# A mixing and expert layer on one core: zero-padded key products, a factored one-hot, and one weight block less

## The chip, the cores and the metric

The kernel runs on one core of a Trainium2 chip. The metric is the device time of one execution in microseconds (us), median of several runs. Below, PE is TensorE (matmuls), PEld its weight loads, DVE VectorE, ACT ScalarE, POOL GpSimd and SP the engine whose queue issues most DMAs.

## The reference

One layer over 512 tokens of width 1024, in float32, cut to what the change touches:

```python
h = rms_norm(x, g_norm1) * (1 + scale1) + shift1
zq, zk, zv, ziq, zik, ziw, zp, zg = split(h @ w_in)
q = rms_norm(zq, 8 heads of 64);  k = rms_norm(zk, one head of 64)
ik = rms_norm(zik, 64);           iq = ziq, 4 heads of 64
score = sum over 4 index heads of iw * relu(iq . ik / 8)      # picks 128 keys per query
attention over the picked keys, 8 heads, one shared key/value head
x = x + gate1 * (merged attention and pooling branches @ w_out)
h2 = rms_norm(x, g_norm2) * (1 + scale2) + shift2
pq = h2 @ w_peer_q              # 8 heads x 2 halves x 64
s = pq half . 128 subkeys of that half;  top 16 of each half, best 16 of their sums
expert = i1 * 128 + i2;  gate = softmax(best 16)             # 8 heads x 16 picks per token
out = x + gate2 * sum over picks of gate * gelu(h2 . u[expert]) * v[expert]
```

## The kernel before

The program has three stretches.

*Mixing* (0 to about 360 us). Weights are split into a high and a low part of a reduced-precision format, so that each product of a weight block (128 outputs, 1024 inputs, 512 tokens) is 24 matmuls of 128x512 (`passes`, lines 168 to 170; `linear` runs a block and loads the next one). Five blocks are computed first, while the adaptive-norm columns still come in (loop from line 254): index key (its 64 columns stored twice), two blocks of index queries, values with index weights, and the key (also stored twice). The four q blocks, four pool blocks and the gate blocks follow. Index scores (`scores`, lines 313 and 314) and logits (lines 432 and 433) are products of two matmuls: one with the high part of the keys, for which the 128 rows hold a head's high part in one half and its low part in the other, and one of 64 rows with the low part of the keys. `heads` makes these 128 rows from a block of two heads. `choose` masks all but the 128 best keys; its steps and the adaptive columns are handed out between blocks by `tick`. Attention runs per token block of 128 and head, with the remaining gate and lift blocks as filling.

*Selection and gates* (about 375 to 754 us). Query blocks are multiplied, `halves` gives scores against 128 subkeys of each half (64 rows each, line 843) and picks the 16 best, `pairs` makes expert numbers and gates. For three of the four token blocks the experts are done densely: `gates` builds, for every token, a 128x128 table of gates. Per 8 tokens VectorE writes two one-hots (lines 615 and 616) and two gated ones (line 621, high and low part of the gate), TensorE multiplies them per token (line 627), and ScalarE copies the result out to `st` (line 628), which goes to memory. Between the groups, steps of `dense_acts` (the products of all 16384 experts' `u` rows, lines 555 to 557, of which 59 blocks are done here) are placed in proportion by `act_until`, the same number for each of the three token blocks.

*Output* (754 us to the end). For each of 128 blocks of experts the gated activations are multiplied with `v` (line 760); the remaining `u` blocks (lines 539 to 541) run beside it, and GpSimd gathers single rows for the fourth token block. Here the order of PE, DVE and ACT is written by hand; in the first two stretches a planner orders the instructions of each engine from the program's order and its own costs. `finish` multiplies by the output gate `g2b`, which is loaded before the last mixing block and kept.

Of the kernel before, what the change touches and what calls it, by code (L numbers as in the profile page):

```python
# [9 lines left out]
F32 = mybir.dt.float32  # L10
# [38 lines left out]
UGAP = 2  # L49
SCALED = 14  # L50
# [12 lines left out]
B_IK, B_IQ, B_VW, B_K, B_Q, B_P, B_GA, B_GP = 0, 1, 3, 4, 5, 9, 13, 21  # L63
# [3 lines left out]
def layer(ctx, tc, xT, cvec, w_ada, cols, consts, w_in, w_grp, w_up, w_out, w_pq, subk, u, uT, v, out):  # L67
# [23 lines left out]
    with ExitStack() as pre:  # L91
# [80 lines left out]
        blocks = [(f"q{i}", w_in[B_Q + i], DT) for i in range(4)]  # L172
# [29 lines left out]
        with ExitStack() as mix:  # L202
# [33 lines left out]
            with tc.tile_pool(name="xp", bufs=1, reuse_waits="tile") as xp, tc.tile_pool(name="xq", bufs=1, reuse_waits="tile") as xq, \  # L236
# [17 lines left out]
                for d in range(DT):  # L254
# [40 lines left out]
            ps = linear("q0", hh, hl)  # L295
            head_norm(ikT, C_GIK, "nik")
            ikl = ak.tile([P, S], F32R, tag="lgs", name="ikl", padded_shape=[P, 16 + S])
            split(ikh, ikl, ikT)
# [7 lines left out]
            def scores(tb):  # L306
                n = (tb + 1) * P
                sc = bias[tb]
                for h in range(NIH):
                    r0 = 64 * (h % 2)  # L310
# [3 lines left out]
                    T.matmul(ps, q[r0:r0 + 64], ikl[r0:r0 + 64, :n], start=False, stop=True)  # L314
# [21 lines left out]
            qsums = pac.tile([P, S], F32, tag="pac", name="nqs")[0:NH, :]  # L336
            for i in range(4):
                nxt = linear(f"q{i + 1}" if i < 3 else "p0", hh, hl)
                if i == 0:
# [3 lines left out]
                    kh, kl = [at.tile([P, S], F32R, tag=f"iq{i}", name=f"k{i}") for i in range(2)]  # L343
                    split(kh, kl, kT)
                queries(i, ps)
# [76 lines left out]
            def attention(tb):  # L422
# [4 lines left out]
                for h in range(NH):  # L427
# [5 lines left out]
                    T.matmul(ps[:, :m], q[r0:r0 + 64], kl[r0:r0 + 64, :m], start=False, stop=True)  # L433
# [50 lines left out]
        g2b = k2.tile([P, D], F32, name="g2b")  # L484
# [7 lines left out]
        nc.sync.dma_start(out=g2b, in_=g2row.to_broadcast([P, D]))  # L492
# [76 lines left out]
    with ExitStack() as win:  # L569
# [415 lines left out]
```

## Time and profile before

| | |
|---|---|
| median of 3 runs | 1576.3 us (1570.9 to 1577.0) |
| profiled execution | 1574.86 us, of which the span is 1573.1 us |
| PE busy | 1530.7 us, 97% |
| PEld busy | 1307.4 us, 83% |
| DVE busy | 1311.7 us, 83% |
| ACT busy | 690.2 us, 44% |
| POOL busy | 324.9 us, 21% |
| mean granted TensorE clock | 0.994 of full speed |

The span runs from the first to the last instruction. Matmuls are pipelined and their ends are modelled, so the starts of matmul rows say more than their durations. Busy shares are means over stretches with different limits.

### The profile page before, as it was taken

What the parts mean: (1) busy time and instruction counts of PE and PEld (TensorE: products, weight loads), DVE (VectorE), ACT (ScalarE), POOL (GpSimd) and SP (SyncE); (2) the same over time, 40 slices, a digit from 0 to 9 for tenths busy, and PEclk for the clock granted to TensorE, in tenths of its full rate; (3) what the DMA queues carried; (4) which work ended last, traced back from release to release, by engine and by line L of the source; (5) the groups of instructions that cost most, each with busy time, mean ns of one, the idle gap of its engine ahead of it and who ended that gap; (6) DMA issues with size and microseconds to landing.
All of it is one profiled execution on the core that took longest, in us unless ns stands there. A gap on an engine that the chain in (4) does not pass through costs nothing.

```text
span 1573.1 us, 22413 instructions
## 1 busy us (share of the span) xinstructions
PE 1530.7 (97%) x7977; PEld 1307.4 (83%) x7977; DVE 1311.7 (83%) x2658; ACT 690.2 (44%) x993; POOL 324.9 (21%) x318
## 2 busy tenths in 40 slices
PE   5999999999999999999999999999999999999998
PEld 3768766786788988899878999999999999998886
DVE  8799767657899999996668888888888888888887
ACT  4543545534346666675334333333333333333332
POOL 0000000000000000000213444444444444443320
PEclk8999999999999999999999999999999999999999
DMA  8412554343135555678999999999999999998884
GB/s 312 169 58 90 206 187 131 105 175 107 68 108 174 184 181 178 207 238 279 330 322 346 328 361 327 346 358 316 361 325 351 358 317 358 322 352 316 310 307 147
DMA packets 158689, 393.91 MB, mean 250 GB/s; under 512 B 13553, under 2 KB 68465, under 8 KB 158578
## 3 DMA queue, kind: packets, MB, share of 16 engines
q1 hardware_dynamic: 121714, 258.26, 46.8%
q0 software_dynamic: 36864, 134.23, 24.2%
q8 instruction: 62, 1.02, 0.3%
q14 instruction: 49, 0.40, 0.1%
HBM read 358.75 MB, written 33.69 MB: 249 GB/s over the span
## 4 chain that ended last, share of the span: by engine, by line
PE 51%; DVE 10%; DMA 2%; ACT 1%; issue 0%; SPq 0%; ACTq 0%; DVEq 0%
PE acc L760 30%; PE pse L541 6%; PE pse L540 6%; PE pse L539 6%; DVE ule L519 2%; DVE oa L621 2%; DMA v<-v 1%; DVE on L615 1%; DVE on L616 1%; PE pse L557 1%; PE pse L556 1%; PE pse L555 1%; DMA g<-gd 0%; PE gm L627 0%; ACT vh L750 0%
## 5 line engine op out<-in xcount | busy, mean ns | idle before, releaser
L691 POOL DMA_INDIRECT ur<-u,ei x128 | 156.7, 1224 | 633.6 <-DMA g<-gd 395.3
L760 PE MATMUL acc<-vl,Wh 128*128 128x512 f32 x768 | 237.1, 390 | 1.0 <-DVE vl L752 1.0
L760 PE MATMUL acc<-vh,Wl 128*128 128x512 f32 x768 | 237.3, 390 | 0.0
L760 PE MATMUL acc<-vh,Wh 128*128 128x512 f32 x768 | 236.8, 389 | 0.0
L699 POOL DMA_INDIRECT vr<-v,ei x128 | 165.2, 1291 | 213.5 <-DVE sacc L704 185.0
L752 DVE TENSOR_TENSOR vl<-v,vh 128x1024 fp32r<-128x1024 f32 x128 | 156.8, 1225 | 59.0 <-ACT vh L750 58.8
L541 PE MATMUL pse<-h2h,ule 128*128 128x384 f32 x552 | 185.2, 336 | 0.2 <-DVE ule L519 0.2
L540 PE MATMUL pse<-h2l,uhe 128*128 128x384 f32 x552 | 184.7, 335 | 0.0
L539 PE MATMUL pse<-h2h,uhe 128*128 128x384 f32 x552 | 184.5, 334 | 0.0
L749 ACT ACTIVATE Wh<-gelu 128x384 fp32r<-128x384 f32 x106 | 55.6, 525 | 291.0 <-PE acc L760 178.3
L760 PEld LDWEIGHTS acc<-vl,Wh 128*128 128x128 f32 x768 | 143.9, 188 | 31.9 <-DVE vl L752 2.1
L760 PEld LDWEIGHTS acc<-vh,Wl 128*128 128x128 f32 x768 | 144.2, 188 | 29.9
L555 PE MATMUL pse<-h2h,uhe 128*128 128x384 f32 x472 | 166.7, 353 | 1.0 <-ACT gelu L564 1.0
L557 PE MATMUL pse<-h2h,ule 128*128 128x384 f32 x472 | 161.5, 343 | 5.3 <-DVE ule L519 5.2
L519 DVE TENSOR_TENSOR ule<-ue,uhe 128x1024 fp32r<-128x1024 f32 x128 | 155.7, 1217 | 12.0 <-ACT uhe L518 12.0
L704 DVE SCALAR_TENSOR_TENSOR sacc<-vr,wt,sacc 128x1024 f32<-128x1024 f32 x127 | 162.7, 1281 | 2.4
L760 PEld LDWEIGHTS acc<-vh,Wh 128*128 128x128 f32 x768 | 143.1, 188 | 24.6 <-ACT vh L750 0.2
L556 PE MATMUL pse<-h2l,uhe 128*128 128x384 f32 x472 | 159.8, 338 | 0.0
L518 ACT ACTIVATE uhe<-ue 128x1024 fp32r<-128x1024 f32 x128 | 134.7, 1053 | 41.4 <-PE pse L556 34.3
L693 DVE SCALAR_TENSOR_TENSOR ur<-ur,hx 128x1024 f32<-128x1024 f32 x128 | 150.6, 1218 | 0.8 <-DMA ur<-u,ei 0.7
L750 ACT ACTIVATE vh<-v 128x1024 fp32r<-128x1024 f32 x128 | 135.9, 1062 | 9.8 <-DMA v<-v 9.4
L628 ACT ACTIVATE st<-gm 128x512 f32<-128x512 f32 x96 | 101.2, 1092 | 54.2 <-PE gm L627 49.8
(412 smaller groups left out, 2757.4 us busy)
## 6 DMA issues: line engine op xcount, KB each, us to landing
ue<-uT SPq DMA_DIRECT2D x128, 512.0 KB, 5.3
v<-v SPq DMA_DIRECT2D x128, 512.0 KB, 5.8
wada<-w_ada SPq DMA_DIRECT2D x48, 512.0 KB, 4.5
gd<-st SPq DMA_DIRECT2D x24, 1024.0 KB, 5.9
g<-gd SPq DMA_DIRECT2D x48, 512.0 KB, 8.0
ad<-gelu SPq DMA_DIRECT2D x22, 192.0 KB, 4.0
wgp<-w_in SPq DMA_DIRECT2D x8, 512.0 KB, 3.6
wga<-w_in SPq DMA_DIRECT2D x8, 512.0 KB, 3.8
```

The lines of the kernel that those rows point to most:

```text
L519: V.tensor_tensor(lo, src, hi.bitcast(F32), op=ALU.subtract)
L539: T.matmul(p, hi[:, k, :], h2h[:, k, :n], start=(k == 0), stop=False)
L540: T.matmul(p, hi[:, k, :], h2l[:, k, :n], start=False, stop=False)
L541: T.matmul(p, lo[:, k, :], h2h[:, k, :n], start=False, stop=(k == DT - 1))
L555: T.matmul(ps, hi[:, k, :], h2h[:, k, :ND], start=(k == 0), stop=False)
L556: T.matmul(ps, hi[:, k, :], h2l[:, k, :ND], start=False, stop=False)
L557: T.matmul(ps, lo[:, k, :], h2h[:, k, :ND], start=False, stop=(k == DT - 1))
L691: G.indirect_dma_start(out=ur, out_offset=None, in_=u, in_offset=bass.IndirectOffsetOnAxis(ap=ei3[:, k:k + 1], axis=0))
L699: G.indirect_dma_start(out=vr, out_offset=None, in_=v, in_offset=bass.IndirectOffsetOnAxis(ap=ei3[:, k:k + 1], axis=0))
L704: V.scalar_tensor_tensor(sacc, vr, wt[:, k:k + 1], sacc, op0=ALU.mult, op1=ALU.add)
L752: V.tensor_tensor(vl, vr, vh.bitcast(F32), op=ALU.subtract)
L760: T.matmul(acc[tb][i], x[:, t], y[:, i * 512:(i + 1) * 512], start=(c == 0 and n == 0), stop=(c == NEXP - 1 and n == 2))
```

## The change

Seven edits. Index key and key are stored in one weight block, and the first q block takes the fifth place of the first loop; the next block is loaded before the constants. The low parts of the two keys are held twice, each with zeros in one half of the 128 rows, so that the second matmul of a score or logit uses 128 rows. The subkeys of both halves are held in one table with zeros, so that `halves` multiplies once per head, with 128 rows and 256 columns. In `gates` the first key is parted into a multiple of 16 and a rest; a one-hot of the 8 multiples is multiplied with the gate, per 32 tokens, and that product with a one-hot of the 16 rests gives the gated one-hot. The copy to `st` runs over tokens innermost, so that four results lie together on the write side and the PSUM side is stepped. The dense steps are placed by `FILL`. `g2b` is loaded in the output loop.

```diff
+KL = 16
+TG = 32
+FILL = (0.36, 0.72, 1.0)
-        blocks = [(f"q{i}", w_in[B_Q + i], DT) for i in range(4)]
+        blocks = [(f"q{i}", w_in[B_Q + i], DT) for i in range(1, 4)]
...
+            q0T = ak.tile([P, S], F32, tag="rel", name="q0T")
-            begin = [(B_IK, ikT), (B_IQ, iqs[:2]), (B_IQ + 1, iqs[2:]), (B_VW, vwT), (B_K, kT)]
+            begin = [(B_KK, (ikT, kT)), (B_IQ, iqs[:2]), (B_IQ + 1, iqs[2:]), (B_VW, vwT), (B_Q, q0T)]
...
+                load_next()
                 nc.sync.dma_start(out=con, in_=consts)
                 for (_, dst), acc in zip(begin, accs):
                     if isinstance(dst, list):
                         heads(dst, acc)
+                    elif isinstance(dst, tuple):
+                        for i, t in enumerate(dst):
+                            for r0 in (0, 64):
+                                A.copy(t[r0:r0 + 64], acc[64 * i:64 * i + 64])
...
-            ps = linear("q0", hh, hl)
+            def split_keys(hi, lows, src):
+
+                A.activation(hi, src, AF.Copy)
+                for j, lo in enumerate(lows):
+                    r, o = slice(64 * j, 64 * j + 64), slice(64 - 64 * j, 128 - 64 * j)
+                    A.activation(lo[o], src[o], AF.Copy, scale=0.0)
+                    V.tensor_tensor(lo[r], src[r], hi[r].bitcast(F32), op=ALU.subtract)
...
                     T.matmul(ps, q, ikh[:, :n], start=True, stop=False)
-                    T.matmul(ps, q[r0:r0 + 64], ikl[r0:r0 + 64, :n], start=False, stop=True)
+                    T.matmul(ps, q, ikl[h % 2][:, :n], start=False, stop=True)
...
                     T.matmul(ps[:, :m], q, kh[:, :m], start=True, stop=False)
-                    T.matmul(ps[:, :m], q[r0:r0 + 64], kl[r0:r0 + 64, :m], start=False, stop=True)
+                    T.matmul(ps[:, :m], q, kl[h % 2][:, :m], start=False, stop=True)
...
-        g2b = k2.tile([P, D], F32, name="g2b")
-        nc.sync.dma_start(out=g2b, in_=g2row.to_broadcast([P, D]))
...
+        tens = kp.tile([P, NEXP // KL, 8], F16, name="tens")
+        V.tensor_copy(tens, iota.rearrange("p (a b) -> p a b", b=KL)[:, :, 0:1].to_broadcast([P, NEXP // KL, 8]))
-        sk = kp.tile([P, NH, P], F32, name="sk")
+        sk = kp.tile([P, NH, 2, P], F32, name="sk")
...
+            ki = oh.tile([P, P], I32, tag="ki", name=f"ki{tb}", bufs=1)
+            V.tensor_copy(ki, keys[:, 0, :])
+            V.tensor_scalar(ki, ki, KL - 1, None, op0=ALU.bitwise_and)
+            V.tensor_copy(low, ki)
+            V.tensor_tensor(keys[:, 0, :], keys[:, 0, :], low, op=ALU.subtract)
...
+                if g * GT % TG == 0:
+                    t = g * GT
+                    rest = oh.tile([P, TG // 2, KL, 2], F16, tag="rest", name=f"rest{tb}_{g}")
+                    V.tensor_tensor(rest, numbers(TG // 2, KL), pairs(low, t, TG).to_broadcast([P, TG // 2, KL, 2]), op=ALU.is_equal)
+                    ten = oh.tile([P, NG, NA, 8], F16, tag="ten", name=f"ten{tb}_{g}")
+                    V.tensor_tensor(ten, tens.unsqueeze(1).to_broadcast([P, NG, NA, 8]), eights(keys[:, 0, :], t), op=ALU.is_equal)
+                    gt = []
+                    for i in range(2):
+                        gt.append(oh.tile([P, NG, NA, 8], F16, tag=f"gt{i}", name=f"gt{i}_{tb}_{g}"))
+                        V.tensor_tensor(gt[i], ten, eights(part[:, i, :], t), op=ALU.mult)
...
-                    V.tensor_tensor(one, numbers, pairs(keys[:, 0, :], t), op=ALU.is_equal)
...
-                        V.tensor_tensor(x, one, pairs(part[:, i, :], t), op=ALU.mult)
+                        V.tensor_tensor(x, gt[i][:, n].rearrange("p a (q j) -> p a q j", j=2).unsqueeze(3).to_broadcast([P, NA, 4, KL, 2]),
+                                        rest[:, 4 * n:4 * n + 4].unsqueeze(1).to_broadcast([P, NA, 4, KL, 2]), op=ALU.mult)
...
-                                T.matmul(ps[:, k, :], two[:, q, :, j], gated[i][:, q, :, j], start=(i == 0), stop=(i == 1))
-                        A.activation(st[:, :, t8 + t4:t8 + t4 + 4].rearrange("p e t -> p t e"), ps, AF.Copy, scale=2.0 ** -SCALED)
+                                T.matmul(ps[:, k, :], two[:, q, :, j], gated[i][:, :, q, :, j], start=(i == 0), stop=(i == 1))
+                        A.activation(st[:, :, t8 + t4:t8 + t4 + 4], ps.rearrange("p k e -> p e k"), AF.Copy, scale=2.0 ** -SCALED)
...
-                act_until(LEAD * DT + between * (tb * steps + n + 1) // (DENSE * steps))
+                f0, f1 = (FILL[tb - 1] if tb else 0.0), FILL[tb]
+                act_until(LEAD * DT + int(between * (f0 + (f1 - f0) * (n + 1) / steps)))
...
+            if a == NEXP + 2:
+                g2b = out_gate()
...
-        for i in range(2):
-            r0 = 64 * i
-            for j in range(2):
-                T.matmul(ps[:, j, :], self.pq[r0:r0 + 64, h + j, tb * P:(tb + 1) * P], self.sk[r0:r0 + 64, h + j, :],
-                         start=True, stop=True)
+        for j in range(2):
+            T.matmul(ps, self.pq[:, h + j, tb * P:(tb + 1) * P], self.sk[:, h + j], start=True, stop=True)
...
-    w = np.concatenate([ik, ik, iq, v, iw, zero, k, k, q, p, g], axis=1)
+    w = np.concatenate([ik, k, iq, v, iw, zero, q, p, g], axis=1)
```

## Rows read from the trace of the kernel before

**Rows 1.** Stretches: us, busy us of PE, PEld, DVE, ACT, POOL, clock, DMA.
```profile
56.00:180.00 124.00, 123.94 (x511) 92.49 (x510) 109.91 (x257) 56.39 (x93) 0.00 (x0) 1.00 0.28 95
180.00:300.00 120.00, 119.71 (x579) 83.41 (x579) 80.38 (x223) 62.96 (x141) 0.00 (x0) 1.00 0.47 152
...
475.00:735.00 260.00, 250.06 (x1894) 228.45 (x1893) 251.79 (x709) 172.50 (x217) 0.00 (x0) 1.00 0.65 201
...
860.00:1573.00 713.00, 707.34 (x3493) 632.96 (x3491) 599.24 (x737) 252.21 (x340) 298.13 (x233) 1.00 0.90 326
```
**Rows 2.** Chain that ended last, in order of time: start, us, what.
```profile
1412.20 149.47 PE acc L760 x659
```

**Rows 3.** PE in order of time, logits of 256 columns: start, us, instruction.
```profile
190.01 0.28 PE L432 MATMUL lg<-k,qs 128*128 128x256 f32 x1
190.22 0.38 PE L433 MATMUL lg<-k,qs 64*128 64x256 f32 x1
190.53 0.38 PE L432 MATMUL lg<-k,qs 128*128 128x256 f32 x1
190.84 0.38 PE L433 MATMUL lg<-k,qs 64*128 64x256 f32 x1
191.15 0.50 PE L169 MATMUL psga<-hl,whga 128*128 128x512 f32 x1
191.49 0.40 PE L170 MATMUL psga<-hh,wlga 128*128 128x512 f32 x1
```

**Rows 4.** The same, logits of 512 columns.
```profile
267.14 0.39 PE L432 MATMUL lg<-k,qs 128*128 128x512 f32 x1
...
268.23 0.39 PE L170 MATMUL psup<-pTh,wlup 128*128 128x512 f32 x1
```

**Rows 5.** Lines L314 and L433: durations min/median/max in ns, starts, shapes.
```profile
L314 PE MATMUL ix<-ikl,iq x12: 379/436/502, 69.6 to 82.7; 64*128 64x256 f32 x4, 64*128 64x384 f32 x4, 64*128 64x512 f32 x4
...
L433 PE MATMUL lg<-k,qs x32: 379/409/492, 180.0 to 276.2; 64*128 64x256 f32 x16, 64*128 64x384 f32 x8, 64*128 64x512 f32 x8
```

**Rows 6.** PE in order of time: first row of block q0, and the row behind its last.
```profile
56.07 0.39 PE L168 MATMUL psq<-hh,whq 128*128 128x512 f32 x1
...
61.51 1.02 PE L291 MATMUL nikps<-niksq,con 128*128 128x512 f32 x2
```

**Rows 7.** PE in order of time around key scores: eight passes, then four.
```profile
611.72 0.72 PE L843 MATMUL ks<-sk,pq 64*128 64x128 f32 x8
612.37 0.45 PE L555 MATMUL pse<-h2h,uhe 128*128 128x384 f32 x1
...
616.74 0.71 PE L843 MATMUL ks<-sk,pq 64*128 64x128 f32 x4
617.37 0.45 PE L555 MATMUL pse<-h2h,uhe 128*128 128x384 f32 x1
```

**Rows 8.** DVE groups by line and shape, 475 to 735 us: busy us, mean ns, idle before.
```profile
L621 DVE TENSOR_TENSOR oa<-on,part 128x1024 f16<-128x1024 f16 x96 | 62.5, 682 | 0.0
L519 DVE TENSOR_TENSOR ule<-ue,uhe 128x1024 fp32r<-128x1024 f32 x45 | 54.7, 1216 | 6.4 <-ACT uhe L518 6.4
L615 DVE TENSOR_TENSOR on<-irep,keys 128x1024 f16<-128x1024 f16 x48 | 32.4, 680 | 0.7 <-ACT keys L602 0.7
...
L864 DVE TENSOR_TENSOR pr<-pr 128x256 bf16<-128x256 bf16 x9 | 2.6, 287 | 0.0
...
L864 DVE TENSOR_TENSOR pr<-k_1h 128x512 bf16<-128x512 bf16 x2 | 0.8, 417 | 0.0
```

**Rows 9.** ACT groups by line and shape, whole span: busy us, mean ns, idle before.
```profile
L628 ACT ACTIVATE st<-gm 128x512 f32<-128x512 f32 x96 | 101.2, 1092 | 54.2 <-PE gm L627 49.8 <-issue 2.5 <-ACT gelu L564 1.0
...
L449 ACT COPY pT<-pt 128x512 f32<-128x512 f32 x8 | 4.6, 580 | 4.9 <-PE pt L447 4.8
```

**Rows 10.** PE's waits from 475 to 735 us: total us, times, longest.
```profile
PE gm L627 <- DVE oa L621: 5.6, 8, 1.8
PE ks L843 <- ACT kss L846: 1.2, 2, 0.8
```

More of the change, by code (lines that the diff above doesn't have):

```diff
@@ L336, in layer @@
             qsums = pac.tile([P, S], F32, tag="pac", name="nqs")[0:NH, :]
+            ps = q0T
             for i in range(4):
                 nxt = linear(f"q{i + 1}" if i < 3 else "p0", hh, hl)
+                queries(i, ps)
                 if i == 0:
@@ L342, in layer @@
                     head_norm(kT, C_GK, "nk")
-                    kh, kl = [at.tile([P, S], F32R, tag=f"iq{i}", name=f"k{i}") for i in range(2)]
-                    split(kh, kl, kT)
-                queries(i, ps)
+                    kh, *kl = [at.tile([P, S], F32R, tag=f"iq{i}", name=f"k{i}") for i in range(3)]
+                    split_keys(kh, kl, kT)
                 tick(2)
@@ L599, in gates @@
             keys = oh.tile([P, 2, P], F16, tag="keys", name=f"keys{tb}", bufs=1)
+            low = oh.tile([P, P], F16, tag="low", name=f"low{tb}", bufs=1)
             part = oh.tile([P, 2, P], F16, tag="part", name=f"part{tb}", bufs=1)
@@ L605, in gates @@
             V.tensor_tensor(part[:, 1, :], gs, part[:, 0, :], op=ALU.subtract)
-            full = [P, 4, NEXP, 2]
-            pairs = lambda x, t: x[:, t:t + 8].rearrange("p (q j) -> p q j", j=2).unsqueeze(2).to_broadcast(full)
-            numbers = irep.unsqueeze(1).to_broadcast(full)
+            ki = oh.tile([P, P], I32, tag="ki", name=f"ki{tb}", bufs=1)
+            V.tensor_copy(ki, keys[:, 0, :])
+            V.tensor_scalar(ki, ki, KL - 1, None, op0=ALU.bitwise_and)
+            V.tensor_copy(low, ki)
@@ L610, in gates @@
+            V.tensor_tensor(keys[:, 0, :], keys[:, 0, :], low, op=ALU.subtract)
+            NA, NG = NEXP // KL, TG // 8
+            pairs = lambda x, t, n: x[:, t:t + n].rearrange("p (q j) -> p q j", j=2).unsqueeze(2)
+            numbers = lambda q, n: irep[:, :n, :].unsqueeze(1).to_broadcast([P, q, n, 2])
+            eights = lambda x, t: x[:, t:t + TG].rearrange("p (g x) -> p g x", x=8).unsqueeze(2).to_broadcast([P, NG, NA, 8])
             for g in range(P // GT):
                 st = oh.tile([P, NEXP, GT], F32, tag="st", name=f"st{tb}_{g}", bufs=STB)
+                if g * GT % TG == 0:
[8 more added lines that the diff above has]
+                        V.tensor_tensor(gt[i], ten, eights(part[:, i, :], t), op=ALU.mult)
@@ L612, in gates @@
                 for t8 in range(0, GT, 8):
                     t = g * GT + t8
-                    one, two = [oh.tile(full, F16, tag=f"on{i}", name=f"on{i}_{tb}_{t}") for i in range(2)]
-                    V.tensor_tensor(one, numbers, pairs(keys[:, 0, :], t), op=ALU.is_equal)
-                    V.tensor_tensor(two, numbers, pairs(keys[:, 1, :], t), op=ALU.is_equal)
+                    full = [P, 4, NEXP, 2]
+                    two = oh.tile(full, F16, tag="on1", name=f"on1_{tb}_{t}")
+                    V.tensor_tensor(two, numbers(4, NEXP), pairs(keys[:, 1, :], t, 8).to_broadcast(full), op=ALU.is_equal)
@@ L705, in sparse, with finish @@
             yield
-    def finish(tb, x, i, half):
+    def finish(g2b, tb, x, i, half):
         c = slice(i * 512, (i + 1) * 512)
@@ L712, in finish, with out_gate @@
         nc.sync.dma_start(out=out[tb * P:(tb + 1) * P, c], in_=x[:, c])
+    def out_gate():
+        t = up.tile([P, DT, P], F32, tag="uh", name="g2b").rearrange("p k e -> p (k e)")
+        nc.sync.dma_start(out=t, in_=g2row.to_broadcast([P, D]))
+        return t
     def residual(tb):
@@ L800, in layer @@
                 for i in range(2):
-                    finish(DENSE, x, i, sacc[:, i * 512:(i + 1) * 512])
+                    finish(g2b, DENSE, x, i, sacc[:, i * 512:(i + 1) * 512])
             if c < NEXP - 2:
@@ L811, in layer @@
                 for i in halves:
-                    finish(tb, xs[tb], i, acc[tb][i])
+                    finish(g2b, tb, xs[tb], i, acc[tb][i])
 class ProductKeys:
@@ L929, in _blocks, with _subkeys @@
     return np.ascontiguousarray(w.reshape(k // P, P, n // P, P).transpose(2, 1, 0, 3))
+def _subkeys(k):
+    s = np.zeros((2, 64, NH, 2, P), k.dtype)
+    for i in range(2):
+        s[i, :, :, i, :] = k[:, i].transpose(2, 0, 1)
+    return s.reshape(P, NH, 2, P)
 def _cols(v):
@@ L965, in arrange @@
         "w_pq": _blocks(w_peer_q[0]),
[L966 removed]
+        "subk": _subkeys(peer_subkeys[0]),
         "u": peer_u[0],
```

20 lines of the change are left out of this document (10 added, 10 removed).

## The prediction

> **What bounds the kernel now.** I read the busy shares by stretch first. TensorE is busy in 123.9 of the 124 us from 56 to 180, in 119.7 of the 120 us of the attention stretch, and in 707 of the last 713 us [rows 1]. A busy matmul row can hide waiting, so I check it by starts. Near the end 659 full matmuls of 512 columns on the critical chain take 149.47 us, 0.227 us each [rows 2], which is 512 columns at the full clock plus 14 ns. From about 860 us nothing but TensorE counts, and the change touches almost nothing there: whatever is won or lost before the first product of the dense output (start at about 754 us) is carried to the end one for one. So the question is how much earlier that point is reached.
>
> Before it there are two kinds of stretch. From 56 to 300 us TensorE never waits by the rows, but it does not always run at 0.227: where a product with 64 rows stands between products with 128 rows, starts are further apart [rows 3, 4]. VectorE is busy 109.9 of 124 us from 56 to 180 and 80.4 of 120 after that, so it is no firm limit there [rows 1]. From 475 to 735 us (the gate tables) VectorE is busy 251.8 of 260 us and TensorE 250.1 [rows 1]: both are near the wall, and the 9.9 us in which TensorE stands still are mostly waits for VectorE's gated one-hots [rows 10].
>
> **The change part by part.**
>
> *Keys in one block.* Index key and key share one weight block, and block q0 goes into the first five. Five blocks still pass through the loop before 56 us, with the same loads and splits, so that part stays. What falls away is the separate q0 after it: 24 matmuls that run from 56.07 to 61.51 us [rows 6], 5.4 us of TensorE time, and one load and one split. The evacuation grows by two half copies and a copy of q0, some 0.6 us each by the ScalarE copy of 128x512 [rows 9], about 1.8 us on an engine that is busy 56 of 124 us there [rows 1]; TensorE has block q1 to run meanwhile. "Next block split early" is what makes that true: its load is issued ahead of the constants on SP's queue, and its split no longer waits for the first `linear`. If q1 were late anyway, a split (1.2 us on VectorE [rows 8]) and ScalarE's part would show, at most 2.5 us. I take 5.4, bounds 3 and 5.4.
>
> *Products over 128 partitions with zeros.* The second half of each score and logit pair now uses all 128 rows with a half of zeros. Two pairs of 256 columns and the full product behind them take from 190.01 to 191.49, 1.48 us, of which the last product but one carries a slow step of 0.34 [rows 3]. Without the change of rows the full product would take 0.23, and four products of 256 columns between 0.12 each (256 columns in the proportion of rows 2) and 0.21 (the one that stands directly behind a full one [rows 3]). So the four and the next take 0.71 to 1.07 in place of 1.14 + 0.34 = 1.48: 0.2 to 0.38 a pair. At 512 columns a pair and the next product take 1.09 us (267.14 to 268.23 [rows 4]) against 3 x 0.23, so 0.40 a pair. There are 12 score pairs and 32 logit pairs [rows 5], half of the logit pairs with 256 columns. I take 0.37: 44 x 0.37 = 16.3 us; bounds 44 x 0.2 = 8.8 and 44 x 0.4 = 17.6. The price is on other engines: two half copies with scale zero on ScalarE and one more half subtraction on VectorE for each of the two keys, about 1.2 + 0.7 us each. They lie before the first scores and before the attention. TensorE has q and pool blocks to run meanwhile; if VectorE, 89% busy from 56 to 180 us [rows 1], is what paces those blocks, the two extra subtractions cost up to 1.4 us. I take 0.
>
> *Key scores of the experts.* Two products of 64 rows per head pair and half become one of 128 rows and 256 columns. A lone group of four passes takes 0.63 us (616.74 to 617.37), but eight passes of both halves together take 0.65 (611.72 to 612.37) [rows 7]: the two row halves of the array run side by side. The new form does the work of four passes in two, with no change of rows: 0.33 (half of the eight) to 0.63. So a group wins 0 to 0.3, for 32 groups 0 to 9.6 us; I take 3, since many groups stand in pairs and VectorE is nearly full there. The Trainium skill speaks against this part: TensorE: Matmul & The Clock Gate, Part 3, (row and column tiling), says that small-K matmuls in distinct row groups run concurrently, and by it zeros in place of a second row group win nothing; the eight passes in 0.65 us agree, and the sum by that rule would be 3 us longer. The table of subkeys doubles to 1 MB, one load ahead of the query weights on SP's queue; the stretch's first weights are already there, so I give it 0 to 1.5 us and take 0.5.
>
> *First key's one-hot factored.* Per group of 8 tokens VectorE issues four pair-mode operations of 1024 fp16 elements at 0.68 us; now three remain (second key's one-hot and the two gated ones), 48 fewer: 48 x 0.68 = 32.7 us. Added per 32 tokens: one of 512 elements (0.42) and three of 256 (0.29) [rows 8], 1.28 us, twelve times 15.3. Added per token block: four operations of 128 elements, below 0.29 each, about 3 us in all. Net 14.4 us less. The new multiply reads a pair (inner step 1, two elements) repeated 16 times, where the old one repeats a pair 128 times, and still writes one contiguous run; I take 0.68 for it. Its other bound is the full-rate price of 1024 elements, 1.22 [rows 8].
>
> VectorE then needs 251.8 - 14.4 = 237 us of these 260. TensorE's work does not shrink, apart from the key scores, so the win ends where TensorE becomes the wall: the 9.9 us of standing still [rows 1, 10] go, and up to 4 us of slow steps behind them. FILL moves dense products from the third token block, where VectorE has air, to the first two, which now can take them. Bounds 4 (waits stay by the in-order queues) and 14.4; I take 10.
>
> *Results written contiguous.* ScalarE's evacuation takes 1.09 us with a step of 64 B on every element written, where plain copies of the same shape take 0.58 [rows 9]. Now four elements lie together on the write side and the step is on the PSUM side. If the read costs nothing it is 0.58, if it costs as much as the write did, about 1.1. ScalarE is busy 172.5 of 260 us [rows 1], so either way it is no wall, and I add nothing. The Trainium skill warns here: PSUM — Partial Sum Buffer, Specifications (TRN2), gives cachelines of 8 bytes and says that any non-contiguous pattern slows matmuls significantly; it speaks of matmuls, and no row here shows a stepped PSUM read. By it the evacuation would stay near 1.1 or go above.
>
> *Output gate.* `g2b` is loaded in the output loop, 512 KB in one load; its first reader comes 29 experts later. On SP's queue it stands among loads of `v`; 0 to 1 us, I take 0.5.
>
> Sum: 5.4 + 16.3 + 3 + 10 - 0.5 - 0.5 = 33.7 us. The profiled execution took 1574.9 us (span 1573.1 and 1.8 around it), 1.4 less than the median of the three runs, 1576.3. 1574.9 - 33.7 = **1541 us**.
>
> **Rivals.** *A, the gates give nothing.* The new multiply is somewhat dearer (0.68 to 0.9), or the evacuation holds the two PSUM buffers, or waits only move. For it: both engines are at the wall, and the order is the planner's. Then 23 to 24 us remain: about 1551, and 1560 if the pairs also sit at their low bound.
>
> *B, the multiply loses the pair mode.* Its first input is no longer one contiguous run: 8 groups x 4 pairs, each repeated 16 times. At 1.22 instead of 0.68 it is 96 x 0.53 = 51 us more on VectorE, 237 + 51 = 288 for a stretch of 260: 29 us longer, less the 24 won before: about 1580, slower or level. It decides once the multiply takes more than about 1.15 us (237 + 96 x 0.47 = 282, which eats the 22 to 24). Against it: pairs with a step of zero outside already run at 0.68 [rows 8].
>
> *C, nothing is won before the gates.* The scores would wait for the longer chain (copies, norm, zeros, split), and TensorE would stand where it now runs slow steps. Against it: no wait between 56 and 300 us, and two q blocks to fill with. Only the gates' 10 us and the block: about 1560.
>
> *D, ScalarE becomes the wall.* 96 evacuations would need over 1.8 us each ((245 - 68) / 96, 68 being the rest of its work there). No row shows a stepped PSUM read, so it isn't excluded, but the stepped write costs 0.5 and this would need 1.2: about 1580.
>
> **How the numbers follow.** Forecast (1528 to 1549) 0.60; A 0.18; C 0.08; B 0.08; D 0.02; something in the planner's order that none of these names, 0.04, half of it slower. The range takes the forecast's bounds (17.6 + 5.4 + 9.6 + 14.4 = 47 us at best, so 1528) and A and C above: **1526 to 1562**. Runs before spread by 6 us, so 0.5% (8 us) is about what can be told from no change. Faster by more: 0.60 + 0.18 + 0.08 + 0.02 = 0.88, less 0.02 for runs of A and C that come to over 1568: 0.86. Within: 0.06. Slower: 0.08.
>
> **What would show it.** Right: a second product of a pair with the spacing of its neighbours, near 0.12 to 0.23 us; no q block alone after the first five; the first product of the dense output at about 720 us instead of 754; the gated multiply at 0.68 and VectorE below 95% busy in the gates; the last stretch unchanged in length. Wrong: the multiply above 0.9 us; new TensorE waits between 56 and 90 us; TensorE waits for VectorE or ScalarE in the gates as long as before; a stall in the output loop near the load of `g2b`.

## The result, and the profile after

The changed kernel takes **1549.5 us** (median of 4 runs, 1548.6 to 1553.4) against 1576.4 before: ratio 0.984, 95% interval 0.981 to 0.987, 26.9 us less. The forecast was 1541 with a range of 1526 to 1562. The direction and the range hold; 7 of the forecast 34 us did not come.

Where it came from is read from the first and last starts of named instructions in both traces, in us from the span's start:

| milestone (PE) | before | after | gained so far |
|---|---|---|---|
| last product of the first five blocks | 55.8 | 55.9 | 0 |
| first score | 68.9 | 71.4 | -2.5 |
| first logit | 179.7 | 177.2 | 2.5 |
| last logit | 276.2 | 262.4 | 13.8 |
| first transpose of the gates | 472.3 | 456.0 | 16.3 |
| first product of the dense output | 754.2 | 729.5 | 24.7 |
| end of the span | 1573.1 | 1547.4 | 25.7 |

So the attention gave 11.3, the gates 8.4, and the stretch up to the first logit only 2.5, although a whole block of 5.4 us is gone from it. The 2.5 us between the last logit and the gates are in part chance: behind a wait of 2.70 us that both traces have there, the granted clock of TensorE was 0.50 from 366.3 to 369.7 us before, and 1.00 after the change; 3.4 us at half the clock cost at most 1.7 (an estimate). The same windows as in [rows 1], of the changed kernel (us, busy us of PE, PEld, DVE, ACT, POOL, clock, DMA):

```profile
56.00:180.00 124.00, 119.58 (x502) 91.39 (x501) 112.22 (x266) 62.36 (x104) 0.00 (x0) 0.97 0.28 95
180.00:300.00 120.00, 119.53 (x627) 91.59 (x626) 89.48 (x233) 68.73 (x151) 0.00 (x0) 1.00 0.51 166
475.00:735.00 260.00, 255.79 (x1881) 237.90 (x1880) 229.53 (x699) 131.93 (x216) 5.04 (x5) 0.99 0.73 225
```

Two things differ in the first two stretches. In 56 to 180 us TensorE, before busy throughout, now stands still for 4.4 us, and its mean clock is 0.97. In 180 to 300 us, where it is busy throughout as before, it issues 627 matmuls where it issued 579 [rows 1].

TensorE in order of time, where it stands still (the bracket is the idle time before the instruction, and what ended it):

```profile
55.94 0.40 PE L173 MATMUL ps<-hh,wls 128*128 128x512 f32 x1
60.76 2.07 PE L300 MATMUL nikps<-niksq,con 128*128 128x512 f32 x2 [4.42 <-ACT niksq L298]
62.62 0.63 PE L318 MATMUL vt<-con,vwT 128*128 128x128 f32 x2
62.91 0.78 PE L171 MATMUL psq<-hh,whq 128*128 128x512 f32 x1
```

And ScalarE in the same time, the engine that it waits for:

```profile
54.29 1.15 ACT L281 COPY ikT<-ps 64x512 f32<-64x512 f32 x2
55.46 1.18 ACT L281 COPY kT<-ps 64x512 f32<-64x512 f32 x2
56.66 1.07 ACT L230 ACTIVATE iq<-ps 64x512 fp32r<-64x512 f32 x2
57.63 0.57 ACT L283 COPY vwT<-ps 128x512 f32<-128x512 f32 x1
58.23 0.59 ACT L230 ACTIVATE iq<-ps 64x512 fp32r<-64x512 f32 x1
58.85 0.58 ACT L283 COPY q0T<-ps 128x512 f32<-128x512 f32 x1
59.46 0.59 ACT L230 ACTIVATE iq<-ps 64x512 fp32r<-64x512 f32 x1
60.07 0.63 ACT L298 ACTIVATE niksq<-ikT 128x512 f32<-128x512 f32 x1
```

`niksq` needs only `ikT`, which is there at 55.4, but it stands behind eight more copies in ScalarE's order. The product that needs it, `nikps` of the index key's norm, stands ahead of block q1 in TensorE's order. Before, q0 was issued first and `nikps` followed at 61.51 [rows 6], five microseconds after its square (ScalarE, then the transpose that follows `nikps` on TensorE, before):

```profile
56.08 0.64 ACT L289 ACTIVATE niksq<-ikT 128x512 f32<-128x512 f32 x1
...
62.37 0.38 PE L301 MATMUL vt<-con,vwT 128*128 128x128 f32 x2
```

What the standing still costs beyond itself is in the clock column of three windows:

```profile
56.40:60.60 4.20, 0.00 (x0) 0.00 (x0) 2.49 (x4) 4.08 (x8) 0.00 (x0) 0.87 0.53 189
60.70:66.10 5.40, 5.34 (x12) 3.20 (x13) 3.04 (x8) 4.68 (x12) 0.00 (x0) 0.50 0.00 0
66.10:70.40 4.30, 4.30 (x19) 3.31 (x17) 2.91 (x6) 2.02 (x5) 0.00 (x0) 0.97 0.00 0
```

TensorE did nothing for 4.2 us, in which its granted clock fell, and for the next 5.4 us it was granted 0.50, its level of 1.2 GHz. In those 5.4 us 12 matmuls start, in the next 4.3 us 19.

The logits of 256 columns, to be held against [rows 3] (start, us, instruction), and the late chain against [rows 2]:

```profile
191.11 0.28 PE L449 MATMUL lg<-k,qs 128*128 128x256 f32 x1
191.23 0.28 PE L450 MATMUL lg<-k,qs 128*128 128x256 f32 x1
191.34 0.28 PE L449 MATMUL lg<-k,qs 128*128 128x256 f32 x1
191.46 0.28 PE L450 MATMUL lg<-k,qs 128*128 128x256 f32 x1
191.58 0.40 PE L172 MATMUL psga<-hl,whga 128*128 128x512 f32 x1
```
```profile
1386.30 149.47 PE acc L805 x659
```

The starts are 0.12 us apart, where they were 0.21 and 0.31; the four products and the way to the next take 0.47 us instead of 1.14. The late chain has the same 659 products in the same 149.47 us.

The gates, VectorE's and ScalarE's groups by line and shape (busy us, mean ns, idle before), against [rows 8, 9], and TensorE's waits from 456 to 701 us, against [rows 10]:

```profile
L658 DVE TENSOR_TENSOR oa<-gt,rest 128x1024 f16<-128x1024 f16 x96 | 62.3, 684 | 0.6 <-PE gm L665 0.5
```
```profile
L666 ACT ACTIVATE st<-gm 128x512 f32<-128x512 f32 x96 | 56.7, 596 | 73.3 <-PE gm L665 63.1 <-issue 6.4 <-ACT st L666 3.1
```
```profile
PE gm L665 <- DVE oa L658: 4.6, 4, 1.8
```

The new multiply takes 0.684 us, as the old one did (0.682). The evacuation takes 0.596 us instead of 1.092: its time went with the stepped write, and the stepped read of PSUM costs 16 ns over a plain copy's 580 [rows 9]. Of the eight waits for `oa` four are left. One thing in this stretch is worse than before: after two waits of 0.6 and 1.2 us the clock falls, where in 475 to 735 us before it stayed at 1.00 [rows 1].

```profile
639.80:643.20 3.40, 3.40 (x28) 2.96 (x27) 3.40 (x6) 1.19 (x2) 0.00 (x0) 0.50 0.25 81
```

### The profile page after: what moved, and what is told of

It is laid out like the page before. It is cut to its first block, busy times and chain, and to the rows that moved or that the text cites. A ratio compares the mean times of both kernels' runs of the same rounds, so it can differ in the third digit from the quotient of the medians.

```text
span 1547.4 us, 22248 instructions
## 1 busy us (share of the span) xinstructions
PE 1504.0 (97%) x7889; PEld 1302.0 (84%) x7889; DVE 1295.0 (84%) x2672; ACT 650.9 (42%) x999; POOL 324.9 (21%) x318
## 4 chain that ended last, share of the span: by engine, by line
PE 87%; DVE 8%; DMA 2%; ACT 2%; issue 1%; SPq 0%; ACTq 0%; DVEq 0%
PE acc L805 32%; PE pse L556 6%; PE pse L555 6%; PE pse L554 6%; PE pse L570 4%; PE pse L572 4%; PE pse L571 4%; PE gm L665 3%; PE po L469 1%; DVE ule L534 1%; PE psga L171 1%; PE psga L172 1%; PE psga L173 1%; PE pso L171 1%; PE psgp L171 1%; PE psgp L173 1%
## 5 line engine op out<-in xcount | busy, mean ns | idle before, releaser
L796 DVE TENSOR_TENSOR Wl<-gelu,Wh 128x384 fp32r<-128x384 f32 x106 | 59.2, 559 | 56.8 <-ACT Wh L794 56.6
```

## The experiments

Times are medians; "beside" is the kernel before in the same runs. A difference from the changed kernel is against its 1549.5. The kernel before lay at 1573.3 to 1574.9 in these runs and at 1576.4 in the first, and the changed kernel was not run again there, so a difference of 1 to 2 us alone says little.

**1. Block q1 ahead of the index key's norm.** `linear("q1")` is issued where `linear("q0")` stood before the change, and q0's heads after the value transposes.

```diff
...
+            ps = linear("q1", hh, hl)
             head_norm(ikT, C_GIK, "nik")
...
-            ps = q0T
-            for i in range(4):
+            queries(0, q0T)
+            for i in range(1, 4):
                 nxt = linear(f"q{i + 1}" if i < 3 else "p0", hh, hl)
                 queries(i, ps)
-                if i == 0:
+                if i == 1:
```

> The changed kernel with block q1 put in program order ahead of the index key's norm, as q0 stood before the change. Theory: the one-block form lost what it won (5.4 us) because the norm's product nikps now stands ahead of q1 on TensorE and waits 4.4 us for ScalarE (its square starts at 60.07 instead of 56.08), after which TensorE runs at a clock below full (0.84 in 60 to 80 us). With q1 in front, TensorE starts q1 at about 56.2, the first score at about 69 (71.4 in the changed kernel) with two q blocks done instead of one: 2.4 + 5.4 = 8 us less, about 1541.5 us in all. Rival 1: the stretch up to 180 us is paced by VectorE (110 of 124 us busy), so the products only wait later and the gain is 0 to 3 us: 1547 to 1550. Rival 2: the stall is filled, but the clock stays low and half is won: about 1545.

1545.6 us (1545.1 to 1547.3), beside 1573.4: 0.982 (0.981 to 0.984). The stall of 4.4 us is gone and the clock stays at 1.00 up to 345 us. TensorE in order of time:

```profile
56.15 0.40 PE L173 MATMUL ps<-hh,wls 128*128 128x512 f32 x1
56.38 0.39 PE L171 MATMUL psq<-hh,whq 128*128 128x512 f32 x1
...
61.83 1.02 PE L300 MATMUL nikps<-niksq,con 128*128 128x512 f32 x2
...
71.75 0.39 PE L332 MATMUL ix<-ikh,iq 128*128 128x256 f32 x1
```

Two q blocks instead of one lie ahead of the first score, but it starts at 71.7 and not 69: the split of q2 came 1.4 us later than that of the second block before (62.84 against 61.48 on ScalarE, behind q0's square and heads), and q0's sum of squares stands ahead of q2 (0.96 us). The first logit starts 5.8 us earlier than in the changed kernel, the gates 4.1, the end 4. So the place is shown, and half of the 8 us came, which is rival 2's number; its reason, a clock that stays low, is not there.

**2. The second products on 64 rows again**, the zeros written and not read:

```diff
-                    T.matmul(ps[:, :m], q, kl[h % 2][:, :m], start=False, stop=True)
+                    T.matmul(ps[:, :m], q[r0:r0 + 64], kl[h % 2][r0:r0 + 64, :m], start=False, stop=True)
```
(and the same for the scores)

> The changed kernel with only the second product of each score and logit pair put back on 64 rows (44 pairs; zeros are still written, and not read). Theory: the change of rows costs 0.37 us a pair, so 16 us more: about 1565 us, the logit stretch (177 to 262 us in the changed kernel) 12 us longer, the second product again with 0.31 us spacing. Rival: the time lies in the copies and norm chain, not in the products, and the pairs are hidden behind VectorE: under 5 us more, below 1555. Low bound of the prediction's own term: 8.8 us more, 1558.

1567.0 us (1566.4 to 1568.5): 17.4 us more for 44 pairs, 0.40 a pair. The slow steps are back (TensorE in order of time):

```profile
191.67 0.28 PE L450 MATMUL lg<-k,qs 128*128 128x256 f32 x1
191.88 0.38 PE L451 MATMUL lg<-k,qs 64*128 64x256 f32 x1
192.19 0.38 PE L450 MATMUL lg<-k,qs 128*128 128x256 f32 x1
192.50 0.38 PE L451 MATMUL lg<-k,qs 64*128 64x256 f32 x1
```

The way from the first logit to the last is 96.3 us instead of 85.2, that from the first score to the last 13.3 instead of 9.0; the gates start 16.4 us later. The zeros are still written here, so this prices the products alone; experiment 10 shows the copies.

**3, 4 and 8. The parts of the gates.** Experiment 3 builds the first key's one-hot whole (two compares and two multiplies for every 8 tokens, no `rest`, `ten`, `gt`); 4 restores the stepped write; 8 does both.

```diff
-                    two = oh.tile(full, F16, tag="on1", name=f"on1_{tb}_{t}")
+                    one, two = [oh.tile(full, F16, tag=f"on{i}", name=f"on{i}_{tb}_{t}") for i in range(2)]
+                    V.tensor_tensor(one, numbers(4, NEXP), pairs(keys[:, 0, :], t, 8).to_broadcast(full), op=ALU.is_equal)
...
+                        V.tensor_tensor(x, one, pairs(part[:, i, :], t, 8).to_broadcast(full), op=ALU.mult)
```
```diff
-                        A.activation(st[:, :, t8 + t4:t8 + t4 + 4], ps.rearrange("p k e -> p e k"), AF.Copy, scale=2.0 ** -SCALED)
+                        A.activation(st[:, :, t8 + t4:t8 + t4 + 4].rearrange("p e t -> p t e"), ps, AF.Copy, scale=2.0 ** -SCALED)
```

> The changed kernel with the first key's one-hot built whole again for every 8 tokens (two compares and two gated multiplies of 1024 elements); the evacuation keeps its contiguous write, FILL its new shares. Theory: VectorE sets the pace of the gates as soon as it gets 14.4 us more (236 busy of 245 us), so the gates grow by the 7 to 8 us that they had shrunk by: about 1557 us. Rival 1: the gates were paced through ScalarE's evacuation, not VectorE: 0 to 2 us more, 1550. Rival 2: with FILL made for the lighter VectorE the old one-hots collide with the dense products in the first two token blocks: 12 us or more, 1562 and up.

> The changed kernel with only the evacuation of the gate products put back: it reads PSUM in order and writes every element 64 B apart. It then takes 1.09 us instead of 0.60. Theory: ScalarE is busy 131 of 252 us in the gates and is no wall, so 48 us more of it cost nothing: 1549 to 1551 us. Rival: two PSUM buffers only, each held 0.5 us longer, so TensorE waits at each of 96 evacuations for a part of it: 4 to 10 us more, 1554 to 1560.

> The changed kernel with both the whole one-hot and the stepped write of the evacuation put back, so the gate tables as before, only FILL and the key scores as changed. Alone the two cost 3.7 and 1.7 us. Theory: they are two reliefs of the same waits (oa to gm to st), each of which suffices for most of the gain, so both together cost more than their sum: 7 to 9 us, 1556 to 1559. Rival: they add up: 5 to 6 us, 1555. Rival 2: the rest of the gates' gain is from key scores and FILL, and both together cost no more than the dearer one: 1553.

Experiment 3: 1553.2 us (1552.0 to 1554.0), 3.7 more. Experiment 4: 1551.2 (1550.5 to 1551.6), 1.7 more. Both: 1556.8 (1553.5 to 1557.6), 7.2 more. Experiment 3 lies between its theory (1557) and its first rival (1550), 4 at its theory, 8 in the range of its theory. TensorE's waits in the gates, of 3, 4 and 8 in this order:

```profile
PE gm L644 <- DVE oa L638: 6.3, 8, 1.8
```
```profile
PE gm L665 <- DVE oa L658: 5.4, 4, 2.1
...
PE gm L665 <- ACT st L666: 1.7, 5, 0.4
```
```profile
PE gm L644 <- DVE oa L638: 8.0, 9, 2.0
```

With the one-hot whole VectorE is busy 244.9 of the 245.7 us from the first gate transpose to the last gate product, against 236.1 of 244.9 in the changed kernel: at the wall, as it was before. Yet the stretch is only 0.8 us longer in this profile, and the first dense-output product comes 2.0 later. The rest lies behind it, in the output loop, where TensorE waits 2.7 us for `vh` and `vl`, the two parts of a block of `v`, and 0.3 us in the changed kernel; experiment 12 shows that loop varying by as much. With the stepped write ScalarE is busy 170 of 247 us, 1.7 us of waits for `st` appear, and the stretch is 1.9 us longer. Both differences come out too small: the changed kernel's profile has the clock of 0.50 from 639.8 to 643.2 us, 8's has a fall like it (637.3 to 640.7), and in 3 and 4 the clock is 1.00 throughout the stretch. With at most 1.7 us for the fall (an estimate), the parts cost up to 2.5 and 3.6 us in the gates. That both together cost more than their sum (7.2 against 5.4 by the medians) is what the theory said, but the traces do not show it. In the profiles 8 is 6.0 us later than the changed kernel at the first dense-output product, and 0.9 of it is there before the gates: about 5 us is what the two are worth in the gates themselves.

**5. Key scores on two halves of 64 rows.**

```diff
...
-            T.matmul(ps, self.pq[:, h + j, tb * P:(tb + 1) * P], self.sk[:, h + j], start=True, stop=True)
+                T.matmul(ps[:, j, :], self.pq[r0:r0 + 64, h + j, tb * P:(tb + 1) * P], self.sk[r0:r0 + 64, h + j, i, :],
+                         start=True, stop=True)
```

> The changed kernel with the experts' key scores put back on two halves of 64 rows (two groups of two products of 128 columns for each head pair and token block, from the same table with zeros). The first experiments left little of the gates' gain to the one-hots (3.7 us more without the factoring) and to the contiguous write (1.7), so this part is asked next. Theory: full-width products win what the rows of key scores bound at 0 to 9.6 us, near the 3 that the prediction took: 1552 to 1554 us. Rival 1: two row halves run side by side (eight passes took 0.65 us), so nothing is won: 1549 to 1550. Rival 2: this part is the larger piece of the gates' 8 us: 1556 or more.

1549.5 us (1548.3 to 1550.2): no difference by the medians, the number of rival 1. TensorE in order of time, first a pair of groups (four products of 128 rows in the changed kernel, then eight of 64 rows in this one):

```profile
599.06 1.08 PE L888 MATMUL ks<-sk,pq 128*128 128x256 f32 x4
599.79 0.52 PE L570 MATMUL pse<-h2h,uhe 128*128 128x384 f32 x1
```
```profile
599.75 0.72 PE L890 MATMUL ks<-sk,pq 64*128 64x128 f32 x8
600.41 0.44 PE L570 MATMUL pse<-h2h,uhe 128*128 128x384 f32 x1
```

The full-width products take 0.73 us and the halves 0.66: zeros buy nothing where the other half of the rows has work of its own. But many groups stand alone, mostly from 366 to 412 us. One of them, in the changed kernel and in this one, with the product behind it:

```profile
377.04 0.59 PE L888 MATMUL ks<-sk,pq 128*128 128x256 f32 x2
377.28 0.58 PE L554 MATMUL pspq<-h2h,uhpq 128*128 128x512 f32 x1
```
```profile
377.42 0.49 PE L890 MATMUL ks<-sk,pq 64*128 64x128 f32 x4
377.84 0.50 PE L554 MATMUL pspq<-h2h,uhpq 128*128 128x512 f32 x1
```

A lone group takes 0.24 us at full width and 0.42 in halves. At the same wait for `ule` (the low part of a block of `u`, split on VectorE) the changed kernel is 1.6 us ahead; then its clock falls and the other's does not (the wait and the clock column behind it, the changed kernel first):

```profile
433.87 0.44 PE L572 MATMUL pse<-h2h,ule 128*128 128x384 f32 x1 [1.85 <-DVE ule L534]
435.00:438.40 3.40, 3.40 (x13) 3.40 (x12) 3.40 (x15) 0.00 (x0) 0.00 (x0) 0.50 0.85 276
```
```profile
435.46 0.44 PE L572 MATMUL pse<-h2h,ule 128*128 128x384 f32 x1 [1.83 <-DVE ule L534]
435.00:438.40 3.40, 2.94 (x17) 2.94 (x18) 3.40 (x6) 0.00 (x0) 0.00 (x0) 1.00 0.53 159
```

Both reach the first gate transpose at 456.0 us. In the gates the same happens: the changed kernel is 0.6 us ahead at the last wait for `oa` (639.17 against 639.75), and its clock falls behind it. So the full-width form is ahead by about 2.2 us in this pair of traces, and two falls of the clock hide it. The other executions have no trace; their mean granted clocks (0.990 to 0.996 in the changed kernel, 0.993 to 0.997 here) point the same way and do not settle it, so what the form is worth at the median stays open between 0 and about 2 us.

**6. The keys in two blocks again**, q0 as a block of its own behind the first five, the next load in its old place:

```diff
...
-            begin = [(B_KK, (ikT, kT)), (B_IQ, iqs[:2]), (B_IQ + 1, iqs[2:]), (B_VW, vwT), (B_Q, q0T)]
+            begin = [(B_IK, ikT), (B_IQ, iqs[:2]), (B_IQ + 1, iqs[2:]), (B_VW, vwT), (B_K, kT)]
...
+            ps = linear("q0", hh, hl)
             head_norm(ikT, C_GIK, "nik")
```

> The changed kernel with index key and key in two blocks again, q0 as a block of its own behind the first five, and the next load in its old place; everything else as changed. Theory: in the changed form the block's 5.4 us went into the 4.4 us stall and the slow clock after it, so that undoing it costs nothing or even wins: first logit at 176 to 178 us as now, 1547 to 1551 us. Rival: the block is worth its 5.4 us and the stall would have come anyway (from the zeros and the longer norm chain): about 1555.

1551.1 us (1549.5 to 1552.5): 1.6 more, at the upper edge of its theory. The first score starts at 69.1 again, 2.3 us ahead of the changed kernel, and the stall and the low clock are gone, so they belong to the one-block form with q1 behind the norm. The first gate transpose comes at 458.5 instead of 456.0. This kernel has a wait that the changed one has not: two logit pairs move forward to 83 us, and at 174.7 TensorE stands 2.4 us for a weight's split on VectorE, which itself stands for a load (as in experiment 9); behind it the clock is 0.50 from 177.7 to 181.1. Without that wait the two-block form might be level or ahead; that was not tried.

**7. Dense products spread evenly** (`FILL` by thirds):

```diff
-FILL = (0.36, 0.72, 1.0)
+FILL = (1 / 3, 2 / 3, 1.0)
```

> The changed kernel with the dense products spread over the three token blocks by thirds again, instead of 0.36, 0.36 and 0.28. Theory: VectorE now has air in all three blocks, so the shares matter little: 1549 to 1551 us. Rival: with thirds the third block, which has no key scores and pair selection of a next one to run, gets too much and the first two stand still in it: 4 us or more, 1553 and up.

1549.3 us (1548.2 to 1550.7): a difference that the runs cannot tell from none, as the theory said.

**9, 11 and 12. Trying to get the rest of the block.** 9 is built on experiment 1: q0's square and heads come after the scores (its copy in a buffer of another pool tag). 11 is 9 without the four background steps behind the first two attention gates. 12 is experiment 1 once more, unchanged.

```diff
...
-            q0T = ak.tile([P, S], F32, tag="rel", name="q0T")
+            q0T = ak.tile([P, S], F32, tag="pT", name="q0T")
...
+                    queries(0, q0T)
+                queries(i, ps)
                 tick(2)
...
             gate(0)
-            tick(2)
             gate(1)
-            tick(2)
```
(the last two minus lines are 11's)

> The kernel with q1 ahead of the index key's norm (which took 1545.6 us), and q0's copy kept in a buffer of its own so that q0's square and heads can come after the scores. With q1 in front the first score still came only at 71.7 us: q2's split stood behind q0's square and heads on ScalarE (started at 62.84), and q0's sum of squares stood ahead of q2 on TensorE (0.95 us). Theory: q2 ends 1 to 2 us earlier and what was won up to the logits (5.8 us there, 4.1 at the end) comes nearer to 8: 1543.5 to 1545 us. Rival: VectorE, busy 29.7 and 30.0 of 30 us in 90 to 120 and 120 to 150, paces the way to the attention, so nothing more is won: 1545.6.

> The kernel with q0's square and heads behind the scores (1551.2 us, slower than the 1545.6 with q1 in front alone), and without the four background steps behind the first two attention gates, so that fewer products of wada stand ahead of the gate weights' split wlga on VectorE. In the last one VectorE stood 2.8 and 0.8 us for wada's load at 168 to 173 us with wlga's split behind it, TensorE then waited 2.5 us and ran at a lower clock. Theory: that order on VectorE is where the gain of the earlier q2 was lost; without it the first product of the dense output comes at 723 to 724 us instead of 727.5, the time is 1543 to 1546 us. Rival: the wait only moves to the next split (the loads are what is late), or the loss is in the output loop (5.8 us longer in that profile): 1548 to 1551.

> The kernel with q1 ahead of the index key's norm once more, unchanged, beside the one above on the same chip: does 1545.6 us and the output loop of 817.5 us from its first product to the end hold? Theory: yes, 1544.5 to 1547, since the loop's products are the same. Rival: the loop's length varies by several us from chip to chip or run to run, and then part of the differences of a few us between these kernels is that: 1549 to 1552.

Experiment 9: 1551.2 us (1548.5 to 1555.3), beside 1574.9; both the theory and its rival are off. The first score comes at 69.6, 2.1 us earlier than in 1, and then it is lost. TensorE, then VectorE, in order of time:

```profile
176.48 0.50 PE L173 MATMUL psga<-hh,wlga 128*128 128x512 f32 x1 [2.46 <-DVE wlga L139]
```
```profile
171.43 1.23 DVE L106 SCALAR_TENSOR_TENSOR wada<-wada,cb 128x1024 f32<-128x1024 f32 x1 [2.79 <-DMA wada<-w_ada]
...
173.45 1.23 DVE L106 SCALAR_TENSOR_TENSOR wada<-wada,cb 128x1024 f32<-128x1024 f32 x1 [0.79 <-DMA wada<-w_ada]
...
175.21 1.22 DVE L139 TENSOR_TENSOR wlga<-wga,whga 128x1024 fp32r<-128x1024 f32 x1
```

Two background products (`wada`, for the adaptive-norm columns) stand ahead of the split of `wlga`, a gate weight's low part, and wait for their loads; behind the stall the clock is 0.58 from 176.4 to 180. In 11 that wait is gone, and the last logit starts at 253.4 (257.0 in 9, 256.1 in 1). But the delayed background work is late for the output projection (`pso`, its product, waits 2.5 us for `who` and 0.9 for `wlo`, the two parts of its weight), the gates start at 457.5, and it takes 1552.4 us (1550.0 to 1552.9). The wait only moved, which is what the rival said, a little above its 1548 to 1551. Experiment 12: 1546.2 us (1544.3 to 1548.8), beside 1574.5: 0.981 (0.980 to 0.983). Its first dense-output product starts at 725.6, as in 1 (725.8); the way from there to the end of the span is 821.4 us in this profile and 817.5 in that of 1. The longer one has 2.0 us of waits for `vh` and `vl`, and behind them a low clock where 1 has 1.00 and 16 matmuls:

```profile
796.89 0.73 PE L807 MATMUL acc<-vh,Wh 128*128 128x512 f32 x2 [1.27 <-ACT vh L797]
...
799.20:802.60 3.40, 3.40 (x10) 2.62 (x9) 3.39 (x6) 0.95 (x2) 1.01 (x1) 0.50 0.79 245
```

So up to that product a profile repeats within 0.2 us, and one such wait with the clock behind it makes nearly all of the 3.9 us after it. Experiment 9 has the same in its loop (3.1 us of waits, 0.50 from 801.6 to 805.0). Of the 5 us between 9 and 12, the trace places 1.9 before that product (727.5 against 725.6). The rest stays open.

**10. The zeros alone, put into the kernel before.**

```diff
...
-            split(ikh, ikl, ikT)
+            split_keys(ikh, ikl, ikT)
...
-                    T.matmul(ps, q[r0:r0 + 64], ikl[r0:r0 + 64, :n], start=False, stop=True)
+                    T.matmul(ps, q, ikl[h % 2][:, :n], start=False, stop=True)
```
(and the same for the keys of the attention)

> The kernel before with the zero halves alone (second products of scores and logits over 128 rows, two copies with scale zero and one more half subtraction per key). Undone alone in the changed kernel they cost 17.4 us. Theory: the pairs win 16 to 17 us in either kernel and the added copies are hidden: about 1557 to 1558 beside a before of 1573.3 to 1574. Rival: the zeros lengthen the chain to the first scores and the two parts only win together, since q0's block stands in the same place: 10 to 13 us, 1561 or more.

1562.1 us (1560.4 to 1563.7), beside 1574.9: 0.991 (0.989 to 0.993), 12.8 less by the medians, which is the rival's number (10 to 13, 1561 or more), and 14.0 by the ratio. The rival's reason is not there: the scores run from 68.9 to 79.4, so they start as before, shrink at once, and their chain is not longer. Part of what was won is lost at 174.5, where TensorE waits 2.3 us for `wlup` and at 180.6 another 0.8 for `wlga` (low parts of a lift and a gate weight), again behind waits of VectorE for the load of `wada`.

## Why the prediction was right, and what was wrong in it

The direction was right for the reason given: TensorE is the bound, what is taken off it before the dense output is carried to the end, and the last stretch changed by 1 us. By its own terms:

- **Zero-padded pairs: 16.3 predicted, 17.4 measured** (experiment 2; 12.8 to 14 in the kernel before, where a new wait took part of it). The spacing of neighbours that was named as the right sign, 0.12 to 0.23 us, is there. The copies and subtractions are hidden (experiment 10: the first score at 68.9 us, as before), and rival C has fallen. The Trainium skill says in TensorEngine Tiling (Array Packing), Key Properties, that a change of tiling mode drains TensorE; it gives no price. The runs fit it, with 0.40 us for each product of 64 rows between products of 128; that the time goes into a drain, no row shows.
- **Keys in one block: 5.4 predicted, 1.6 measured** (experiment 6), and that with a wait in the other kernel that has nothing to do with the block; up to the first score, ahead of that wait, the one-block form is 2.3 us behind. This is the step that failed: "TensorE has block q1 to run meanwhile". It had q1 ready, and could not run it: `nikps` was ahead of it in TensorE's order, since the change moved `linear` behind `head_norm`, and ScalarE's queue had grown by half copies and q0's. The stall of 4.4 us and the clock of 0.50 after it took what the block gave. For the clock: the way from `nikps` to the first transpose took 1.86 us instead of 0.86 (61.51 [rows 6] to 62.37), and six products of q1 with two transposes 3.19 instead of about 1.6, so an estimate of 2.6 us; with the stall 7.0, against 5.4 won. q0's sum of squares, another 0.95 us (70.42 to 71.37), stands ahead of the first score. The text counted the copies' time (1.8 us) and left out who stands behind them. Its sign for "wrong" was the right one: a new wait of TensorE between 56 and 90 us. Experiment 1 wins back 5.8 us up to the first logit and 4 at the end.
- **Key scores: 3 predicted, 0 measured by the medians** (experiment 5), **about 2.2 in the traces by the last wait of the gates**, which two falls of the clock take back. The sum took one range, 0 to 0.3 us, for every group. A pair of groups loses 0.07 us, a lone one wins 0.18 or more. The rule named there, the Trainium skill's TensorE: Matmul & The Clock Gate, Part 3, on row tiling, made the sum 3 us longer. The trace agrees with it for pairs (0.73 against 0.66 us); a lone group has no second row group beside it.
- **Gates: 10 predicted, 7.2 measured** (experiment 8; about 5 of it in the gates themselves). The multiply kept its 0.68 us, so rival B is out, and A too, by which the gates would have given nothing. VectorE fell to 236 of 245 us. TensorE is now busy 238.8 of those 244.9; of its 9.9 us of standing still [rows 1] about 4 went. The prediction let all of it go, but four waits for `oa` remain, three at the starts of the token blocks and one at 614.58 us, and the clock of 0.50 from 639.8 takes up to 1.7 more, a term the sum did not have. The evacuation was costed at nothing; the runs give 1.7 us by the medians and, by the estimate above, up to 3.6 in the gates.
- **The two small costs, 0.5 each.** No wait stands at the table of subkeys or at `g2b`, whose load landed 9.0 us after its issue at 1378.3, well ahead of its first reader at 1519.7.

Sum of the parts as measured by the medians: 17.4 + 1.6 + 0 + 7.2 = 26.2 of the 26.9 us, with an uncertainty of 1 to 2 us in each. That it comes so near is partly luck, since each part was undone alone and met waits and falls of the clock of its own.

The version that beats both kernels is experiment 1: 1545.6 and 1546.2 us in two sets of runs, 28 us below the kernel before.

## What to carry to other kernels

A short product that changes the number of rows among full ones costs a step each time (0.40 us on average here), and zeros over all rows remove it; where two row halves run as neighbours (eight passes in 0.66 us here) zeros gain nothing. When a block of work is taken away, look at what its time covered: walk the in-order queue of the engine that is to gain, find the first instruction that needs the result of another engine, and read that engine's queue up to there. A stall of 4 us is priced with the low clock behind it, and a stretch filled tighter may meet the next late load: follow the gain to the end of the trace. Before a difference of a few microseconds between two profiles is explained, compare their clock columns stretch by stretch.

## What the runs showed that was not expected

- After 4.2 us without a matmul TensorE's granted clock was 0.50 for 5.4 us, and after a stall of 2.5 us 0.58 for the next 3.6 us. Shorter waits did it too, and not each time: behind the same wait of about 1.8 us for `ule`, ahead of the gates, the clock fell to 0.50 for 3.4 us in the changed kernel (435.0) and in experiment 3 (435.5), and stayed at 1.00 in 4 and 5.
- A stepped read of PSUM by ScalarE costs next to nothing (596 ns for 128x512, plain copy 581), while a stepped write of the same shape into SBUF takes 1,089 (experiment 4). The Trainium skill's PSUM — Partial Sum Buffer, Specifications (TRN2), warns of non-contiguous patterns for matmuls; for ScalarE's read the runs show no such price.
- A change of a few microseconds in one place let the planner's order shift elsewhere: in experiments 6, 9, 10 and 11 logit pairs moved forward by some 90 us, and a weight's split came to stand behind loads that were late by up to 2.8 us.
